# Differential attention on one core: context scores in the transpose and output banks

## The chip, the cores and the metric

One core of a Trainium2 chip runs the kernel. The metric is the device time of one execution in microseconds (us): the median of three runs of the kernel before is 1611.29 us (1610.94 to 1612.96).

## The reference

Two layers of a backbone with three token mixers in parallel. Each layer has 128 context tokens and 512 latent tokens, 640 columns in all. The mixer that the change touches is differential attention: 4 heads, each with two score maps of 64 channels,

```python
p = softmax(q1 k1 / 8) - lam * softmax(q2 k2 / 8)      # per head
o = p v
```

Context tokens read the 128 context keys only. Latent tokens read 512 latent and 256 cached keys, 768 in all. The output of a head then goes through an RMS norm per token. Beside it run a state-space mixer and a neighbourhood attention of 8 heads. All inputs are normalised and projected from one matrix, and the three results are merged by gates and projected again.

## The kernel before

Everything lies feature by token: 128 features on the partitions, 640 tokens along the free axis. Each float32 operand of a projection is split into a high and a low part and takes three matmuls (`feat`, line 163, matmul at line 175; a full projection of 128 features is 48 matmuls of 320 columns).

A layer runs the state-space mixer, then differential attention (`diff_attn`, line 496, once for each of 4 heads), then neighbourhood attention (`na_vkq`, `na_ctx`, `na_head`, 4 pairs of heads), then the last merges and the output projection. `build` (lines 1202 to 1233) puts projections that depend on none of these between the heads: keys and queries of the next head (`diff_kq`), a gate (`gate_in`), merge logits (`logits`, counts in `LA`, `LN`, `LC`), merges. Below they are called fill.

The order in which each engine gets its instructions is fixed at build time by a planner, which takes each engine's instructions by their place in the program as soon as they are ready in its own timeline. Tiles of one tag share that tag's buffers; a new tile waits until the one before it in the buffer is released.

PSUM has 8 banks. Three rotate for projections (tag `mm`, line 161). One bank, tag `t`, takes transposes; one, tag `o`, takes outputs (both from the pool `pp`). The last three are one tile, tag `s` (`bank3`, line 520), for the scores of a query tile: two maps of 768 columns.

A head goes like this. Context: scores of both maps into `s` (line 526); `soft` takes the maximum of both maps in one reduction (line 510), the exponentials (line 513, into the tiles `e0` and `e1`, one buffer each), and the difference of the maps (line 517); a transpose into `t` (line 529), its copy `px` (line 531), the output matmul into `o` (line 533), its copy into `of` (line 534). Then `after_ctx` runs `diff_out` of the previous head, which uses `o` twice (line 602). Then four latent query tiles: scores into `s` (lines 547 and 551), `soft`, two rounds of three transposes through `t` (line 558, copied at 560 and 561), and for each two query tiles 18 output matmuls into `o` (line 566), copied at line 568.

Between head h and head h+1 the program has `diff_norm` of head h (line 1212, body from line 571). It squares the head's output (line 576), sums the squares into `o` (line 201), makes the factor through VectorE and GpSimd, transposes it into the same `o` tile (line 591) and reads that at line 593, which is the tile's last reader. So in program order `o` goes: outputs of head h, `diff_norm` of head h, context output of head h+1, `diff_out` of head h.

Of the kernel before, what the change touches and what calls it, by code (L numbers as in the profile page):

```python
# [9 lines left out]
F32 = mybir.dt.float32  # L10
F32R = mybir.dt.float32r
AF = mybir.ActivationFunctionType
ALU = mybir.AluOpType
AX = mybir.AxisListType
# [110 lines left out]
class Net:  # L125
# [370 lines left out]
    def diff_attn(self, l, h, v, kq, nlam, p, cp, ps, pp, after_ctx):  # L496

        nc = self.nc
        half = (slice(0, 64), slice(64, 128))
        j = h % 2  # L500
        vh, vl, vx = v
        ks, qh, ql, kx, qx = kq
        of = cp.tile([128, NT], F32, tag="of", name="of", bufs=4)
        zz = cp.tile([128, 5, 2], F32, tag="zz", name="zz", bufs=2)

        def soft(s, n, t):

            st = p.tile([128, 4], F32, tag="st", name="st", bufs=3)
            e = [p.tile([128, 768], F32, tag=f"e{m}", name="e", bufs=1)[:, 0:n] for m in range(2)]
            nc.vector.tensor_reduce(out=st[:, 0:2], in_=s, axis=AX.X, op=ALU.max)  # L510
            nc.vector.tensor_scalar(out=st[:, 0:2], in0=st[:, 0:2], scalar1=-0.125, scalar2=None, op0=ALU.mult)  # L511
            for m in range(2):
                nc.scalar.activation(e[m], s[:, m], AF.Exp, bias=st[:, m:m + 1], scale=0.125, accum_out=zz[:, t, m:m + 1])  # L513
            nc.vector.reciprocal(st[:, 2:3], zz[:, t, 1:2])
            nc.vector.tensor_scalar(out=st[:, 3:4], in0=st[:, 2:3], scalar1=zz[:, t, 0:1], scalar2=nlam, op0=ALU.mult,
                                    op1=ALU.mult)
            nc.vector.scalar_tensor_tensor(out=e[0], in0=e[1], scalar=st[:, 3:4], in1=e[0], op0=ALU.mult, op1=ALU.add)
            return e[0]

        def bank3():  # L520
            return ps.tile([128, 1536], F32, tag="s", name="s")


        s = bank3().rearrange("p (b n) -> p b n", b=3)[:, 0:2, 0:128]
        for m in range(2):
            nc.tensor.matmul(s[:, m, :], lhsT=qx[half[m], :], rhs=kx[half[m], :], start=True, stop=True)
        e = soft(s, 128, 0)
        pt = pp.tile([128, 4, 128], F32, tag="t", name="t")
        nc.tensor.transpose(pt[:, 0, :], e, self.ident)
        px = p.tile([128, 128], F32, tag="px", name="px")  # L530
        nc.scalar.activation(px, pt[:, 0, :], AF.Copy)
        ov = pp.tile([128, 512], F32, tag="o", name="o")
        nc.tensor.matmul(ov[:, 0:128], lhsT=vx[:, j * 128:(j + 1) * 128], rhs=px, start=True, stop=True)
        nc.scalar.activation(of[:, 0:128], ov[:, 0:128], AF.Copy)
        after_ctx()

        for qp in range(2):
            ph = p.tile([128, 6, 256], F32R, tag="ph", name="ph")
            pl = p.tile([128, 6, 256], F32R, tag="pl", name="pl")
            for qi in range(2):  # L540
                qt = 2 * qp + qi
                s = bank3()
                qs = slice(qt * 128, (qt + 1) * 128)
                for m in range(2):
                    c0 = (512, 0)[m]
                    for i, q in enumerate((qh[m], ql[m])):
                        nc.tensor.matmul(s[:, m * 768 + c0:m * 768 + c0 + 256], lhsT=q[:, qs], rhs=ks[m][:, c0:c0 + 256],  # L547
                                         start=(i == 0), stop=(i == 1))
                    c0 = (0, 256)[m]
                    for i, q in enumerate((qh[m], ql[m])):  # L550
                        nc.tensor.matmul(s[:, m * 768 + c0:m * 768 + c0 + 512], lhsT=q[:, qs], rhs=ks[m][:, c0:c0 + 512],  # L551
                                         start=(i == 0), stop=(i == 1))
                e = soft(s.rearrange("p (m n) -> p m n", m=2), 768, 1 + qt)
                for b in range(2):
                    pt = pp.tile([128, 4, 128], F32, tag="t", name="t")
                    for i in range(3):
                        kt = 3 * b + i
                        nc.tensor.transpose(pt[:, i, :], e[:, kt * 128:(kt + 1) * 128], self.ident)  # L558
                    dst = (slice(None), slice(3 * b, 3 * b + 3), slice(qi * 128, qi * 128 + 128))
                    nc.scalar.activation(ph[dst], pt[:, 0:3, :], AF.Copy)  # L560
                    nc.vector.tensor_tensor(out=pl[dst], in0=pt[:, 0:3, :], in1=ph[dst], op=ALU.subtract)  # L561
            ov = pp.tile([128, 512], F32, tag="o", name="o")
            for kt in range(6):
                sv = slice(j * 128, (j + 1) * 128)
                for n, (x, q) in enumerate(((vh, ph), (vh, pl), (vl, ph))):
                    nc.tensor.matmul(ov[:, 0:256], lhsT=x[:, kt, sv], rhs=q[:, kt, :], start=(kt == 0 and n == 0),  # L566
                                     stop=(kt == 5 and n == 2))
            nc.scalar.activation(of[:, 128 + qp * 256:384 + qp * 256], ov[:, 0:256], AF.Copy)
        return of, zz
# [719 lines left out]
```

## Time and profile before

| what | value |
|---|---|
| median of 3 runs | 1611.29 us |
| the profiled execution's own time | 1611.84 us |
| its span | 1610.1 us |
| TensorE matmul busy | 1583.1 us, 98% |
| VectorE busy | 1064.1 us, 66% |
| ScalarE busy | 774.1 us, 48% |
| differential attention, layer 0 | about 252 to 484 us of the span |
| neighbourhood attention, layer 0 | about 487 to 731 us of the span |

Times in rows are microseconds from the span's start. PE is TensorE's matmul, ACT ScalarE, DVE VectorE, POOL GpSimd. A matmul's busy time includes the pipeline, so neighbouring matmuls overlap; the distance between their starts is what a matmul costs in a stream.

### The profile page before, as it was taken

What the parts mean: (1) busy time and instruction counts of PE and PEld (TensorE: products, weight loads), DVE (VectorE), ACT (ScalarE), POOL (GpSimd) and SP (SyncE); (2) the same over time, 40 slices, a digit from 0 to 9 for tenths busy, and PEclk for the clock granted to TensorE, in tenths of its full rate; (3) what the DMA queues carried; (4) which work ended last, traced back from release to release, by engine and by line L of the source; (5) the groups of instructions that cost most, each with busy time, mean ns of one, the idle gap of its engine ahead of it and who ended that gap; (6) DMA issues with size and microseconds to landing.
All of it is one profiled execution on the core that took longest, in us unless ns stands there. A gap on an engine that the chain in (4) does not pass through costs nothing.

```text
span 1610.1 us, 29172 instructions
## 1 busy us (share of the span) xinstructions
PE 1583.1 (98%) x11371; PEld 1508.3 (94%) x11371; DVE 1064.1 (66%) x2299; ACT 774.1 (48%) x1790; POOL 155.8 (10%) x182
## 2 busy tenths in 40 slices
PE   8999999999999999999999999999999999999998
PEld 5999899999999999999989989999999999999998
DVE  5865688667556566756677667676575575577565
ACT  4535654344445555443455466334444555454342
POOL 2003421011000000000000252101010000000000
PEclk9999999999999999999999999999999999999999
DMA  9663225321225343436543222452122543344543
GB/s 340 210 244 112 89 93 160 125 75 56 85 88 162 127 127 110 151 115 245 185 164 133 85 75 82 139 174 74 60 89 78 161 127 89 112 133 155 207 168 131
DMA packets 81673, 214.63 MB, mean 133 GB/s; under 512 B 9728, under 2 KB 25664, under 8 KB 80512
## 3 DMA queue, kind: packets, MB, share of 16 engines
q1 hardware_dynamic: 80624, 211.46, 40.1%
q8 instruction: 90, 1.47, 0.4%
q0 software_dynamic: 480, 0.88, 0.2%
q10 hardware_dynamic: 432, 0.43, 0.1%
q14 instruction: 47, 0.39, 0.1%
HBM read 170.27 MB, written 34.08 MB: 127 GB/s over the span
## 4 chain that ended last, share of the span: by engine, by line
PE 89%; DVE 4%; DMA 3%; ACT 1%; issue 1%; POOL 1%; SPq 0%; DVEq 0%; ACTq 0%; POOLq 0%
PE mm L175 61%; PE mm L187 7%; PE s L1001 2%; PE o L1025 2%; PE o L566 2%; PE t L1017 2%; PE ex L175 2%; PE s L551 1%; PE g L813 1%; PE t L558 1%; DMA aw<-in_w_ada 1%; PE y L826 1%; PE y L268 1%; PE s L547 1%; DMA qd<-qr 1%
## 5 line engine op out<-in xcount | busy, mean ns | idle before, releaser
L175 PE MATMUL mm<-hl,hi 128*128 128x320 f32 x1856 | 577.8, 311 | 0.8 <-DVE hl L383 0.8
L175 PE MATMUL mm<-hh,hi 128*128 128x320 f32 x1856 | 574.5, 310 | 3.3 <-ACT hh L382 2.8
L175 PE MATMUL mm<-hh,lo 128*128 128x320 f32 x1856 | 573.5, 309 | 0.2 <-DVE lo L151 0.2
L175 PEld LDWEIGHTS mm<-hh,hi 128*128 128x128 f32 x1856 | 348.4, 188 | 11.6 <-ACT hh L382 4.1
L175 PEld LDWEIGHTS mm<-hh,lo 128*128 128x128 f32 x1856 | 348.9, 188 | 7.3 <-issue 4.7
L175 PEld LDWEIGHTS mm<-hl,hi 128*128 128x128 f32 x1856 | 348.5, 188 | 6.3 <-issue 2.6
L151 DVE TENSOR_TENSOR lo<-raw,hi 128x1024 fp32r<-128x1024 f32 (+2 forms) x194 | 235.6, 1215 | 93.7 <-ACT hi L150 90.7
L150 ACT ACTIVATE hi<-raw 128x1024 fp32r<-128x1024 f32 (+2 forms) x194 | 200.1, 1032 | 177.5 <-PE mm L175 116.5
L175 PE MATMUL mm<-yh,hi 128*128 128x320 f32 x320 | 98.8, 311 | 1.1 <-DVE th L1080 0.7
L175 PE MATMUL mm<-yl,hi 128*128 128x320 f32 x320 | 99.0, 310 | 0.0
L175 PE MATMUL mm<-yh,lo 128*128 128x320 f32 x320 | 99.0, 310 | 0.0
L187 PE MATMUL mm<-hi,hh 128*128 128x264 f32 (+1 forms) x320 | 90.5, 284 | 1.8 <-DVE vl L423 1.7
L187 PE MATMUL mm<-lo,hh 128*128 128x264 f32 (+1 forms) x320 | 91.0, 285 | 0.0
L187 PE MATMUL mm<-hi,hl 128*128 128x264 f32 (+1 forms) x320 | 90.6, 284 | 0.0
L560 ACT ACTIVATE ph<-t 128x384 fp32r<-128x384 f32 x64 | 31.4, 490 | 113.9 <-PE t L558 113.9
L175 PE MATMUL mm<-mgh,hi 128*128 128x320 f32 x256 | 78.7, 311 | 1.7 <-ACT hi L150 1.7
L175 PE MATMUL mm<-mgl,hi 128*128 128x320 f32 x256 | 79.9, 312 | 0.0
L175 PE MATMUL mm<-mgh,lo 128*128 128x320 f32 x256 | 78.7, 309 | 1.0 <-DVE lo L151 1.0
L510 DVE TENSOR_REDUCE st<-s 128x2 f32<-128x1536 f32 (+1 forms) x40 | 59.5, 1487 | 25.6 <-PE s L551 24.0
L1018 ACT ACTIVATE ph<-t 128x512 fp32r<-128x512 f32 x64 | 38.3, 598 | 68.4 <-PE t L1017 68.0
L513 ACT ACTIVATE e<-s,st 128x768 f32<-128x768 f32 (+1 forms) x80 | 62.8, 795 | 15.1 <-DVE st L511 15.1
L561 DVE TENSOR_TENSOR pl<-t,ph 128x384 fp32r<-128x384 f32 x64 | 35.5, 554 | 49.9 <-ACT ph L560 49.4
(351 smaller groups left out, 3052.8 us busy)
## 6 DMA issues: line engine op xcount, KB each, us to landing
raw<-in_w_feat SPq DMA_DIRECT2D x110, 512.0 KB, 3.6
aw<-in_w_ada SPq DMA_DIRECT2D x8, 2048.0 KB, 8.2
raw<-in_w_out SPq DMA_DIRECT2D x32, 512.0 KB, 3.6
thd<-th SPq DMA_DIRECT2D x48, 320.0 KB, 2.2
th<-thd SPq DMA_DIRECT2D x48, 320.0 KB, 3.7
raw<-in_w_br SPq DMA_DIRECT2D x24, 512.0 KB, 3.5
accd<-th SPq DMA_DIRECT2D x32, 320.0 KB, 2.8
ac<-accd SPq DMA_DIRECT2D x32, 320.0 KB, 4.3
```

The costliest lines, as they stand in the source:

```text
L150: nc.scalar.activation(hi, raw, AF.Copy)
L151: nc.vector.tensor_tensor(out=lo, in0=raw, in1=hi, op=ALU.subtract)
L175: nc.tensor.matmul(ps, lhsT=s, rhs=r, start=(k == 0 and n == 0), stop=(k == K - 1 and n == 2))
L187: nc.tensor.matmul(ps, lhsT=s, rhs=r, start=(k == 0 and q == 0), stop=(k == 7 and q == 2))
L510: nc.vector.tensor_reduce(out=st[:, 0:2], in_=s, axis=AX.X, op=ALU.max)
L513: nc.scalar.activation(e[m], s[:, m], AF.Exp, bias=st[:, m:m + 1], scale=0.125, accum_out=zz[:, t, m:m + 1])
L561: nc.vector.tensor_tensor(out=pl[dst], in0=pt[:, 0:3, :], in1=ph[dst], op=ALU.subtract)
L566: nc.tensor.matmul(ov[:, 0:256], lhsT=x[:, kt, sv], rhs=q[:, kt, :], start=(kt == 0 and n == 0), stop=(kt == 5 and n == 2))
L1001: nc.tensor.matmul(s[:, c0:c0 + n], lhsT=q[:, i * 128:(i + 1) * 128], rhs=ks[j][:, k0:k0 + n], start=(x == 0), stop=(x == 1))
L1017: nc.tensor.transpose(pt[:, t, :], e[:, t * 128:(t + 1) * 128], self.ident)
L1018: nc.scalar.activation(ph[:, i], pt, AF.Copy)
L1025: nc.tensor.matmul(out, lhsT=lw, rhs=sel(q), start=(first and x == 0), stop=(last and x == 1))
```

## The change

The context scores of a head no longer use the three-bank tile `s`. Map 0 goes into a tile of tag `t`, map 1 into a tile of tag `o`. `soft` takes a list of two tiles in this case, and reduces each with an instruction of its own. Latent scores stay in `s`.

```diff
-            nc.vector.tensor_reduce(out=st[:, 0:2], in_=s, axis=AX.X, op=ALU.max)
+            if isinstance(s, list):
+                for m in range(2):
+                    nc.vector.tensor_reduce(out=st[:, m:m + 1], in_=s[m], axis=AX.X, op=ALU.max)
+            else:
+                nc.vector.tensor_reduce(out=st[:, 0:2], in_=s, axis=AX.X, op=ALU.max)
+                s = [s[:, m] for m in range(2)]
             nc.vector.tensor_scalar(out=st[:, 0:2], in0=st[:, 0:2], scalar1=-0.125, scalar2=None, op0=ALU.mult)
             for m in range(2):
-                nc.scalar.activation(e[m], s[:, m], AF.Exp, bias=st[:, m:m + 1], scale=0.125, accum_out=zz[:, t, m:m + 1])
+                nc.scalar.activation(e[m], s[m], AF.Exp, bias=st[:, m:m + 1], scale=0.125, accum_out=zz[:, t, m:m + 1])
...
-        s = bank3().rearrange("p (b n) -> p b n", b=3)[:, 0:2, 0:128]
+        s = [pp.tile([128, 512], F32, tag=t, name=t)[:, 0:128] for t in ("t", "o")]
         for m in range(2):
-            nc.tensor.matmul(s[:, m, :], lhsT=qx[half[m], :], rhs=kx[half[m], :], start=True, stop=True)
+            nc.tensor.matmul(s[m], lhsT=qx[half[m], :], rhs=kx[half[m], :], start=True, stop=True)
```

## Rows read from the trace of the kernel before

**Rows 1.** The page, part 1, TensorE: busy us, share of span, instructions.
```profile
PE 1583.1 (98%) x11371; PEld 1508.3 (94%) x11371; DVE 1064.1 (66%) x2299; ACT 774.1 (48%) x1790; POOL 155.8 (10%) x182
```

**Rows 2.** Windows of both layers' differential attention: window, length, busy us by engine.
```profile
250.00:460.00 210.00, 207.30 (x1452) 199.44 (x1451) 143.04 (x280) 95.62 (x199) 20.42 (x18) 1.00 0.33 100
...
1025.00:1260.00 235.00, 230.48 (x1601) 220.96 (x1600) 152.47 (x289) 101.48 (x212) 26.32 (x20) 1.00 0.31 97
```

**Rows 3.** Timeline, layer 0, head 0 to 1: start us, us, engine, line, operation.
```profile
325.79 0.39 ACT L568 ACTIVATE of<-o 128x256 f32<-128x256 f32 x1 [0.86 <-PE o L566]
326.07 0.27 ACT L531 ACTIVATE px<-t 128x128 f32<-128x128 f32 x1
326.23 0.74 ACT L576 ACTIVATE sq<-of 128x640 f32<-128x640 f32 x1
...
329.42 0.90 ACT L513 ACTIVATE e<-s,st 128x768 f32<-128x768 f32 x1 [2.45 <-DVE st L511]
...
331.83 1.02 DVE L517 SCALAR_TENSOR_TENSOR e<-e,st 128x768 f32<-128x768 f32 x1
...
335.50 0.49 PE L558 MATMUL t<-masks,e 128*128 128x128 f32 x3
...
337.23 0.55 DVE L561 TENSOR_TENSOR pl<-t,ph 128x384 fp32r<-128x384 f32 x1
...
339.73 0.49 PE L558 MATMUL t<-masks,e 128*128 128x128 f32 x3
...
339.93 0.81 DVE L593 TENSOR_TENSOR rows<-o,five 10x640 fp32r<-10x640 f32 x1 [0.96 <-PE o L591]
...
340.65 0.90 ACT L513 ACTIVATE e<-s,st 128x768 f32<-128x768 f32 x1
...
343.45 0.38 PE L533 MATMUL o<-px,vx 128*128 128x128 f32 x2
```

**Rows 4.** Timeline, layer 1, head 2 to 3, the last such place.
```profile
1220.15 0.38 ACT L568 ACTIVATE of<-o 128x256 f32<-128x256 f32 x1 [1.23 <-PE o L566]
...
1221.76 0.91 ACT L513 ACTIVATE e<-s,st 128x768 f32<-128x768 f32 x1 [0.43 <-DVE st L511]
...
1230.22 0.80 DVE L593 TENSOR_TENSOR rows<-o,five 10x640 fp32r<-10x640 f32 x1
...
1231.07 0.49 PE L533 MATMUL o<-px,vx 128*128 128x128 f32 x2 [0.17 <-DVE rows L593]
```

**Rows 5.** Timeline of TensorE, layer 1, context of head 2.
```profile
1154.90 0.49 PE L526 MATMUL s<-kx,qx 64*128 64x128 f32 x4
...
1158.53 0.27 PE L529 MATMUL t<-masks,e 128*128 128x128 f32 x1
```

**Rows 6.** One line's instructions: ns min/median/max, first and last start. Lines 510, 975.
```profile
L510 DVE TENSOR_REDUCE st<-s x40: 411/1751/1759, 253.3 to 1249.2; 128x2 f32<-128x1536 f32 x32, 128x2 f32<-128x256 f32 x8
...
L975 DVE TENSOR_REDUCE st<-s x16: 280/286/292, 487.9 to 1447.1; 128x1 f32<-128x128 f32 x16
```

**Rows 7.** Timeline of ScalarE, end of differential attention, layer 0.
```profile
464.03 0.43 ACT L1061 ACTIVATE th<-mm 128x320 f32<-128x320 f32 x1
466.49 0.28 ACT L892 ACTIVATE early<-mm 128x128 f32<-128x128 f32 x1 [2.03 <-PE mm L175]
...
484.46 0.39 ACT L568 ACTIVATE of<-o 128x256 f32<-128x256 f32 x1 [1.45 <-PE o L566]
```

**Rows 8.** Timeline of TensorE and VectorE, end of neighbourhood attention, layer 0.
```profile
719.02 0.60 PE L1017 MATMUL t<-masks,e 128*128 128x128 f32 x4
...
720.28 0.69 DVE L1019 TENSOR_TENSOR pl<-t,ph 128x512 fp32r<-128x512 f32 x1 [0.56 <-ACT ph L1018]
...
723.80 0.60 PE L1017 MATMUL t<-masks,e 128*128 128x128 f32 x4
...
725.13 0.30 PE L175 MATMUL mm<-yh,hi 128*128 128x320 f32 x1
...
727.77 0.39 PE L1025 MATMUL o<-ph,vs 128*128 128x512 f32 x1
```

**Rows 9.** One head's window by tile, `s`, `t`, `o` in turn; columns PE, PEld, DVE, ACT.
```profile
312.00:370.00 58.00, 7.08 (x36) 5.08 (x36) 7.42 (x5) 8.29 (x20) 1.00 0.27 81
312.00:370.00 58.00, 4.80 (x28) 3.37 (x28) 4.63 (x9) 4.70 (x10) 1.00 0.27 81
312.00:370.00 58.00, 7.83 (x51) 6.67 (x51) 2.04 (x4) 1.05 (x3) 1.00 0.27 81
```

**Rows 10.** Windows where the output projection starts: busy by engine, PEclk, DMA share.
```profile
764.00:768.00 4.00, 2.79 (x16) 2.00 (x14) 2.88 (x7) 2.98 (x5) 0.00 (x0) 1.00 0.29 96
768.00:780.00 12.00, 11.85 (x71) 11.85 (x72) 7.06 (x13) 4.12 (x6) 0.00 (x0) 0.86 0.58 182
```

## The prediction, as put on record before the result

> **What bounds the kernel now.** I read the page's table of engines first: TensorE is busy 98% of the span, the next engine 66% [rows 1]. So the time changes only if TensorE stands idle longer or shorter. The windows by stage come next: in the two stretches of differential attention TensorE idles 210.00 − 207.30 = 2.7 us and 235.00 − 230.48 = 4.5 us [rows 2]. That is 7.2 us for all that a shorter chain of heads could give back there.
>
> TensorE is full because fill stands between the steps of a serial chain: scores, softmax, transposes, outputs, tile after tile and head after head, then the same for neighbourhood attention. Differential attention's own matmuls are 7.08 + 4.80 + 7.83 = 19.7 us of a head's 58 us, about a third (a little less, since fill overlaps them) [rows 9]; the rest is fill. The reader must therefore look at two things: how long the chain is, and whether there is fill for its whole length.
>
> **What the change takes away.** Context scores no longer hold `s`, so the first latent scores of a head can be made, and their maxima taken, while the context softmax runs. What that can give is bounded by the 7.2 us of idle time and, below, by nothing; I put it at 0 alone, because today these scores wait little where TensorE has fill, and because of what comes next.
>
> **What it adds in instructions.** Eight context softmaxes (4 heads, 2 layers) reduce twice 286 ns instead of once 411 ns [rows 6]: 0.16 us each, 1.3 us of VectorE in all. VectorE is idle a third of the time; hidden, and at most 1.3 us if not. The score matmuls are the same.
>
> **What it adds in waits.** This is the large term. The score of map 1 now needs `o`. Between a head's last outputs and the next head's context the program gives `o` to `diff_norm`. That buffers of a tag go round in program order is to be read from the trace: at the first change of heads `o` is copied out from 325.79 to 326.18, the context's `px` is there at 326.34, and the squares that `diff_norm` sums are there only at 326.97; yet the context output (line 533) runs at 343.45, after the norm's last reader (339.93 + 0.81 = 340.74) [rows 3]. At the last change TensorE even stands still before line 533 until line 593 is done [rows 4]. Of six such changes (heads 0 to 1, 1 to 2, 2 to 3, two layers) these are the first and the last. Today this costs nothing: the context output is not in the chain, and the head's latent tiles go on. After the change the *scores* of the context wait there, and behind them the context softmax; and since `e0` and `e1` have one buffer each, the first latent exponential waits behind the context's transpose. Behind line 526 on TensorE's queue stand the fill and the first latent scores; the planner can put them ahead of it, so that the wait is the chain's and not the queue's. Who waits is ScalarE, with the exponentials, and through them every later tile of the head. No DMA is added or moved.
>
> The price of one change of heads, from the end of the output copy to the first latent exponential:
> - Today: 329.42 − 326.18 = 3.2 us at the first [rows 3], 1221.76 − 1220.53 = 1.2 us at the last [rows 4].
> - Afterwards: `o` is held for 340.74 − 326.18 = 14.6 us [rows 3] down to 1231.02 − 1220.53 = 10.5 us [rows 4]. Then the context: from its scores to the end of its transpose 1158.80 − 1154.90 = 3.9 us, where nothing was in the way [rows 5], with 0.2 us for the second reduction. Then 0.4 us until the exponential, as from the transposes' end at 340.22 to 340.65 [rows 3]; its maxima are ready.
> - So longer by at least 10.5 + 3.9 + 0.2 + 0.4 − 3.2 = 11.8 us and at most 14.6 + 4.5 − 1.2 = 17.9 us. I take the middle, 15 us: with the softmax out of the way VectorE serves the norm sooner, but the norm's five small steps and its two trips over TensorE remain.
>
> Three changes of heads in a layer: the chain is 45 us longer (35 to 54). The first head of a layer has no norm before it and costs nothing.
>
> **What covers it.** TensorE goes on with fill that the program has later. But the fill of differential attention ends with the last logit at 464.03; at 466.49 TensorE is already in the projections of neighbourhood attention, while the last head's output is copied at 484.46 [rows 7]. And what is taken from there is missing at the end of neighbourhood attention, where there is none over: the logits run out at 725.13, when the first merge operand appears, 2.6 us before the chain's last outputs at 727.77 [rows 8]. So in each layer some 45 us of fill are lacking in all, at the end of differential or of neighbourhood attention.
>
> **What the lack costs.** Not 45 us, because the chain is quicker where no fill stands in it. One tile takes 340.65 − 329.42 = 11.2 us from exponential to exponential. Of these, the first transposes start 2.65 us after their input (332.85 to 335.50) and the second 1.95 us after theirs (337.78 to 339.73) [rows 3]: by itself the tile would take 6.6 us, 0.6 of it. In neighbourhood attention transposes are 4.8 us apart and the second stand ready from 720.97, 2.8 us early [rows 8], so by that step 0.4; I use 0.6 for both. If 45 us of fill are two thirds of a stretch, the stretch is 67 us long as it is spaced now; by itself 0.6 x 67 = 40 us; TensorE's own work in it is 22 us; idle 18 us. The chain enters each of the two stretches some 2.5 us ahead of TensorE (the delays above), which takes off 5 us: 13 us in a layer, 26 us in all.
>
> Ends: 35 us lacking at 0.5 gives 26 − 17 − 5 = 4 us in a layer, 8 in all; 54 us at 0.8 gives 65 − 27 − 5 = 33 us, 66 in all. Added to the profiled execution's 1611.84 us the forecast is 1638; its time is 0.55 us above the median of the runs, so I put 1637 us, with its own range 1619 to 1660.
>
> **A rule on the clock.** At the start of the output projection TensorE is busy 2.79 of 4 us, and in the next 12 us its granted clock averages 0.86, so part of them was at the lower level, 1.2 GHz, against 2.4 GHz before [rows 10]. The Trainium skill, TensorE: Matmul & The Clock Gate, section Part 1: The HAM clock gate, says that the slower clock is what an engine gets that has lately had little to do. By that rule, with which these rows agree, stretches without fill run at half clock; it is the second rival below.
>
> **Rivals.**
> 1. *The delays swallow it.* The chain's lead of 2 to 3 us at every TensorE step [rows 3, 8] might absorb the lack all along, since order and not latency rules a full engine. For it: TensorE waits hardly at all today. Against: at the last change of heads it did wait for the norm [rows 4], so there the lead was used up. Time 1608 to 1614.5.
> 2. *Half clock.* TensorE's 22 us of own work in the stretches become 44 us, more than the 40 us of the chain: 22 us lost in a layer, with no lead to take off, 44 in all: 1655 us. If nothing at all were hidden, 2 x 54 = 108 us: 1719. For it: the rows just named. Against: idle and busy alternate in such a stretch, and a slower TensorE fills itself.
> 3. *Faster: the freed `s` decides.* If the planner gives `o` to the context's scores before the norm, they run at once and latent scores stand ready behind them; the chain gets shorter and TensorE's idle 7.2 us [rows 2] shrink: 1604 to 1608 us. It decides as soon as `o` does not go round in program order. Against: the two changes of heads shown.
> 4. *Nothing happens*: the norm gets so quick without the softmax beside it that `o` is free when the context comes. It would have to fall from 10.5 us to about 2; one GpSimd step and two trips over TensorE lie in it. I count this with the first.
>
> **How the numbers follow.** Forecast (a longer chain, partly uncovered) 0.54; rival 2 0.13; rivals 1 and 4 0.18; rival 3 0.15. What a measurement here can tell from no change is 0.2%, 3.2 us. Slower: 0.54 + 0.13 = 0.67; same 0.18; faster 0.15. The range for 8 in 10 goes from 1607, which leaves out about half of rival 3, to 1668, which leaves out the upper half of rival 2 and the tail of the forecast.
>
> **What would show it.** In the changed kernel: line 526 comes after line 593 at the six changes of heads, and the first latent exponential some 16 us after the copy of the outputs, not 1 to 3; line 547 of a head's first tile comes before or beside line 526; the last logits are done before the last transposes of neighbourhood attention, with bare gaps between transposes there; TensorE's busy time about the same and its idle time 20 to 30 us longer, in the last third of differential attention and at the end of neighbourhood attention. The prediction is wrong if line 526 comes before line 593, or if it comes after and TensorE's idle time does not grow.

## The result, and the profile after

The changed kernel takes 1673.95 us (median of 4 runs, 1671.71 to 1676.5) against 1611.12 us of the kernel before beside it: a ratio of 1.0385, with an interval of 1.0372 to 1.0399. It is 62.8 us slower. The direction and the wait for the bank `o` were forecast, the size was not: 1637 us was predicted, 1668 us was the upper end.

Lines behind the change are numbered 5 higher than before (526 is now 531, 568 is 573, 593 is 598, 513 is 518); the second reduction is line 512, the latent one 514.

Part 1 of the page, which answers to [rows 1]: busy us, share of the span, instructions.

```profile
PE 1613.6 (96%) x11371; PEld 1530.1 (91%) x11371; DVE 1069.5 (64%) x2307; ACT 774.7 (46%) x1790; POOL 158.5 (9%) x182
```

The span is 1673.5 us, 63.4 longer. The same 11371 matmuls are busy 30.5 us longer, and TensorE stands still 59.9 instead of 27.0 us, 32.9 more. So the loss has two halves, and the reader must look for both.

The first change of heads in layer 0, from the timeline of the changed kernel; it answers to [rows 3].

```profile
323.95 0.49 PE L531 MATMUL t<-kx,qx 64*128 64x128 f32 x2
...
324.06 0.38 ACT L573 ACTIVATE of<-o 128x256 f32<-128x256 f32 x1 [2.23 <-PE o L571]
...
324.48 0.74 ACT L581 ACTIVATE sq<-of 128x640 f32<-128x640 f32 x1
...
324.69 1.75 DVE L514 TENSOR_REDUCE st<-s 128x2 f32<-128x1536 f32 x1
...
328.41 1.17 PE L201 MATMUL o<-masks,sq 128*128 128x1 f32 x10
...
336.75 0.81 DVE L598 TENSOR_TENSOR rows<-o,five 10x640 fp32r<-10x640 f32 x1
...
338.02 0.48 PE L531 MATMUL o<-kx,qx 64*128 64x128 f32 x2
...
339.49 0.36 ACT L518 ACTIVATE e<-o,st 128x128 f32<-128x128 f32 x1
...
342.19 0.27 PE L534 MATMUL t<-masks,e 128*128 128x128 f32 x1
...
343.52 0.27 ACT L536 ACTIVATE px<-t 128x128 f32<-128x128 f32 x1
...
343.68 0.91 ACT L518 ACTIVATE e<-s,st 128x768 f32<-128x768 f32 x1
```

The predicted order stands there step by step. The maxima of the first latent tile are taken at 324.69 (line 514), and its exponential waits until 343.68: behind the norm's last reader (336.75), the score of map 1 (338.02), the context softmax and its transpose (342.19). From the end of the output copy (324.44) that is 19.2 us; before it was 3.2. It is so at all six changes: map 1 goes into `o` 10 to 17 us after map 0 into `t`, and each time after the norm's last reader. The line's instructions, two for each change; first and last start:

```profile
L531 PE MATMUL t<-kx,qx x12: 272/322/374, 324.0 to 1272.5; 64*128 64x128 f32 x12
...
L531 PE MATMUL o<-kx,qx x12: 272/322/373, 338.0 to 1284.4; 64*128 64x128 f32 x12
```

From the end of the copy to the first latent exponential the six changes take 19.2, 22.7, 14.0, 20.3, 22.0 and 18.0 us; before they took 3.2, 1.2, 2.4, 3.1, 3.8 and 1.2. That is 16.9 us more on average. I call this the wait at a change of heads; the experiments are compared by the sum of the six, which rises from 14.9 to 116.3 us.

Now where TensorE loses. Windows of layer 0 from the first head's context on, cut at the start of head 1's context, at the first neighbourhood score and at the last outputs; columns as in [rows 2]. First the kernel before:

```profile
252.00:312.00 60.00, 59.73 (x411) 58.21 (x410) 44.40 (x85) 25.07 (x50) 3.24 (x4) 1.00 0.50 155
312.00:487.40 175.40, 172.97 (x1223) 166.24 (x1222) 108.63 (x206) 81.38 (x174) 17.18 (x14) 1.00 0.27 84
487.40:731.00 243.60, 243.60 (x1728) 238.11 (x1728) 153.40 (x386) 123.58 (x317) 2.73 (x2) 1.00 0.41 129
```

Then the kernel after, cut at the same events:

```profile
252.00:324.00 72.00, 72.00 (x499) 70.46 (x498) 53.22 (x103) 29.57 (x57) 7.00 (x7) 1.00 0.47 147
324.00:514.50 190.50, 175.94 (x1163) 165.60 (x1162) 101.27 (x188) 75.97 (x163) 15.97 (x12) 0.96 0.22 67
514.50:761.50 247.00, 242.85 (x1702) 236.61 (x1702) 154.78 (x389) 124.94 (x321) 2.71 (x2) 0.99 0.41 131
```

The layer is 509.5 − 479.0 = 30.5 us longer for the same work, 3364 against 3362 matmuls. TensorE's idle time rises from 0.27 + 2.43 + 0 to 0 + 14.56 + 4.15, by 16.0 us. The other 14.5 us are busy time: a matmul in 324.0 to 514.5 takes 175.94 / 1163 = 0.1513 us instead of 0.1414. Of this the slower clock, shown next, can be at most 10.2 us: 20.5 us of the layer were at the lower level, none before. No run splits the rest. Only 26 of 1728 matmuls moved from neighbourhood attention to differential attention.

Part of why the same matmuls are slower shows at the end of head 1, in TensorE's timeline of the changed kernel:

```profile
371.75 0.49 PE L563 MATMUL t<-masks,e 128*128 128x128 f32 x3
373.75 0.55 PE L563 MATMUL t<-masks,e 128*128 128x128 f32 x3 [1.51 <-DVE pl L566]
376.64 0.39 PE L552 MATMUL s<-ks,qh 128*128 128x256 f32 x1 [2.34 <-ACT e L518]
...
382.00 0.41 PE L571 MATMUL o<-ph,vl 128*128 128x256 f32 x1
...
387.34 1.69 PE L201 MATMUL o<-masks,sq 128*128 128x1 f32 x10 [2.05 <-ACT sq L581]
...
389.24 0.41 PE L187 MATMUL mm<-lo,hh 128*128 128x256 f32 x1
...
395.21 0.31 PE L175 MATMUL mm<-hh,lo 128*128 128x320 f32 x1
```

and in windows of the stretch with the first two gaps, of the stretches behind them and behind the third, and of one behind a single gap of 1.90 us at 448.39; the third column from the end is the granted clock:

```profile
371.75:376.64 4.89, 1.04 (x8) 0.56 (x6) 2.79 (x6) 2.75 (x6) 0.00 (x0) 1.00 0.00 0
376.60:385.00 8.40, 7.76 (x33) 6.50 (x34) 2.57 (x5) 1.19 (x3) 0.00 (x0) 0.59 0.00 0
...
387.34:396.00 8.66, 8.66 (x46) 8.61 (x46) 4.51 (x14) 2.39 (x3) 1.17 (x1) 0.61 0.09 20
...
450.29:458.50 8.21, 8.05 (x51) 7.42 (x52) 3.13 (x5) 2.15 (x4) 0.00 (x0) 1.00 0.31 106
```

Between and behind the transposes of a tile TensorE has nothing (1.51 and 2.34 us), and after the outputs it waits for the squares (2.05 us). Behind these gaps it works at 1.2 GHz most of the time: an output matmul takes 0.21 us from start to start and not 0.12, and so does each matmul of the value projection until 394. Not every gap has this behind it: the clock stayed at 2.4 GHz behind the single gap of 1.90 us, and in the kernel before behind one of 1.72 us at 375.26. What stands before the fall at 377.8 is 4.89 us in which TensorE was busy for 1.04. Over the execution 63.3 us are at the lower level, against 10.6 before; at half speed that is at most 26.4 of the 30.5 us of longer busy time. The Trainium skill, TensorE: Matmul & The Clock Gate, section Part 1: The HAM clock gate, has the slower clock follow on little activity; the first two windows agree.

What TensorE waits for, in the changed kernel: us in total, times, longest.

```profile
PE s L552 <- ACT e L518: 10.3, 6, 2.3
PE mm L175 <- ACT th L1066: 5.2, 8, 1.3
PE o L201 <- ACT sq L581: 4.1, 3, 2.0
...
PE t L563 <- DVE pl L566: 3.2, 3, 1.5
```

The first, third and fourth are short waits of the chain's own steps, next to which no fill was ready; the first was 1.7 us in all before. The second is of projections that wait until ScalarE has read an earlier result out of a bank. The wait of map 1 itself is hardly among them (1.0 us), since the fill goes on there.

### The profile page after: what moved, and what is told of

Same layout as the page of the kernel before. It is cut to its first block, busy times and chain, and to the rows that moved or that the text cites. A ratio compares the mean times of both kernels' runs of the same rounds, so it can differ in the third digit from the quotient of the medians.

```text
span 1673.5 us, 29181 instructions
## 1 busy us (share of the span) xinstructions
PE 1613.6 (96%) x11371; PEld 1530.1 (91%) x11371; DVE 1069.5 (64%) x2307; ACT 774.7 (46%) x1790; POOL 158.5 (9%) x182
## 4 chain that ended last, share of the span: by engine, by line
PE 90%; DVE 3%; ACT 3%; DMA 3%; issue 1%; POOL 0%; SPq 0%; DVEq 0%; ACTq 0%; POOLq 0%
PE mm L175 61%; PE mm L187 7%; PE o L571 2%; PE s L1006 2%; PE o L1030 2%; PE t L1022 2%; PE s L556 2%; PE ex L175 2%; PE t L563 1%; DMA aw<-in_w_ada 1%; PE g L818 1%; PE y L831 1%; PE s L552 1%; PE y L268 1%; ACT e L518 1%
## 5 line engine op out<-in xcount | busy, mean ns | idle before, releaser
L565 ACT ACTIVATE ph<-t 128x384 fp32r<-128x384 f32 x64 | 31.3, 490 | 122.3 <-PE t L563 122.3
L566 DVE TENSOR_TENSOR pl<-t,ph 128x384 fp32r<-128x384 f32 x64 | 35.4, 553 | 59.8 <-ACT ph L565 59.3
L514 DVE TENSOR_REDUCE st<-s 128x2 f32<-128x1536 f32 x32 | 56.1, 1753 | 27.3 <-PE s L556 27.1
L187 PEld LDWEIGHTS mm<-hi,hh 128*128 128x128 f32 x320 | 62.4, 195 | 2.3 <-ACT th L1066 1.5
```

What stands on the lines that cost most here:

```text
L187: nc.tensor.matmul(ps, lhsT=s, rhs=r, start=(k == 0 and q == 0), stop=(k == 7 and q == 2))
```

## The experiments

Eleven kernels were run, each beside runs of the kernel before, against whose median its time is taken here. Beside it stands the sum of the six waits at a change of heads, in one profiled execution of each. It goes with the large losses at about one rate; the small ones it does not order. Two profiles of the changed kernel differ by 3 us in it:

| kernel | sum of six waits, us | more than before | time over the kernel before, us | per us of wait |
|---|---|---|---|---|
| before | 14.9 | | | |
| norm late, old banks | 16.5 | 1.6 | 6.8 | 4 |
| two reductions, old banks | 21.1 | 6.2 | 5.0 | 0.8 |
| projection banks | 28.8 | 13.9 | 17.3 | 1.2 |
| values unblocked, old banks | 34.1 | 19.2 | 15.2 | 0.8 |
| `t` and `s` | 52.9 | 38.0 | 21.2 | 0.56 |
| norm behind the context | 59.8 | 44.9 | 29.2 | 0.65 |
| values unblocked | 111.4 | 96.5 | 60.8 | 0.63 |
| the change, again | 113.3 | 98.4 | 60.9 | 0.62 |
| busy in the gaps | 115.1 | 100.2 | 64.2 | 0.64 |
| the change | 116.3 | 101.4 | 62.8 | 0.62 |
| logits earlier | 122.3 | 107.4 | 73.1 | 0.68 |
| `s` and `o` | 150.5 | 135.6 | 70.2 | 0.52 |

**Norm behind the context.** The changed kernel with the norm of heads 0 to 2 put behind the next head's context, so that map 1 finds `o` free.

```diff
-                                d = self.diff_norm(att, cp, pp)
+                                d = self.diff_norm(att, cp, pp) if h == 3 else None
...
-                                pend.append(lambda ...: self.diff_out(l, h, att, d, g, sg, pp))
+                                pend.append(lambda ...: self.diff_out(l, h, att, self.diff_norm(att, cp, pp) if d is None else d, g, sg, pp))
```

> The changed kernel, with the norm of heads 0 to 2 placed behind the next head's context (just ahead of its output step) and not ahead of it; banks as changed. Theory A, the context scores wait for the output bank behind the norm: line 531 comes right after the head's last outputs, the first latent exponential 5 to 8 us after the output copy instead of 19 to 24, and the time falls from 1674 to 1600 to 1615 us. Rival B, the transpose bank held by a context map, or two reductions, or the freed three-bank tile itself cost the time: 1650 us or more.

1643.32 us, a ratio of 1.0183 (1.0165 to 1.0201). Between the two expectations: with the norm out of the way about half of the loss goes, not all. A wait of 8 to 12 us stays at each change of heads.

**One bank each.** Which of the two banks costs?

```diff
-        s = [pp.tile([128, 512], F32, tag=t, name=t)[:, 0:128] for t in ("t", "o")]
+        s = [pp.tile([128, 512], F32, tag="t", name="t")[:, 0:128], bank3()[:, 512:640]]
```

> The changed kernel, with context map 0 in the transpose bank and map 1 in the three-bank score tile; nothing waits for the output bank. Theory A: 1606 to 1617 us, as before the change. Rival B, the transpose bank is what costs: 1650 us or more.

```diff
+        s = [bank3()[:, 0:128], pp.tile([128, 512], F32, tag="o", name="o")[:, 0:128]]
```

> The changed kernel, with context map 0 in the three-bank score tile and map 1 in the output bank. Theory A: the whole loss stays, or more, since the score tile is now held while the norm runs: 1665 to 1695 us. Rival B, the transpose bank: 1606 to 1617 us.

With `t` and `s` 1635.36 us, 1.0137 (1.0121 to 1.0153); with `s` and `o` 1684.36 us, 1.0434 (1.0403 to 1.0466). The second met its first theory, the first missed both: with no wait for `o` a loss of 21 us remains. Its timeline at the first change of heads:

```profile
326.55 0.48 PE L531 MATMUL t<-kx,qx 64*128 64x128 f32 x2
...
326.66 0.38 ACT L573 ACTIVATE of<-o 128x256 f32<-128x256 f32 x1 [0.72 <-PE o L571]
...
328.57 0.37 ACT L518 ACTIVATE e<-t,st 128x128 f32<-128x128 f32 x1 [0.76 <-DVE st L516]
...
337.43 0.90 ACT L518 ACTIVATE e<-s,st 128x768 f32<-128x768 f32 x1 [0.38 <-DVE st L516]
```

Map 0 needs `t` back from the previous head's last transposes (read until 323.35), so the context starts where the head before ends. In the kernel before it had been done beside that head's last tile:

```profile
312.11 0.49 PE L526 MATMUL s<-kx,qx 64*128 64x128 f32 x4
```

This wait the prediction did not see. And with map 1 in `s` the latent scores are late again, which is what the change had meant to avoid, so the 21 us are not the price of `t` alone. The timeline of `s` and `o`:

```profile
325.36 0.39 ACT L573 ACTIVATE of<-o 128x256 f32<-128x256 f32 x1 [0.72 <-PE o L571]
...
337.75 0.81 DVE L598 TENSOR_TENSOR rows<-o,five 10x640 fp32r<-10x640 f32 x1 [0.37 <-PE o L596]
...
340.72 0.48 PE L531 MATMUL o<-kx,qx 64*128 64x128 f32 x2
...
349.62 0.90 ACT L518 ACTIVATE e<-s,st 128x768 f32<-128x768 f32 x1 [0.17 <-DVE st L516]
```

Here `s` is held until map 1 has come, the latent scores follow that, and the wait is 23.9 us. That is 7 to 9 us more time than the full change takes, in which `s` is free but map 0 waits for `t`; the two are not parted here.

**Logits earlier.** If fill lacks at the changes of heads, more of it there should help.

```diff
-LA = ((), (1, 2), (3,), (4, 5, 6))
+LA = ((), (1, 2, 3, 4), (), (5, 6))
```

> The changed kernel, with logits 3 and 4 of the first merge placed at head 1, ahead of the second value projection, instead of at heads 2 and 3. In the changed kernel TensorE has no fill from 371.9 to 388.9 us: value columns fill the three projection banks and wait for the value tile that head 1 still reads. Theory C, fill is there but blocked at that place: two more logits (14 us of matmuls) ahead of the block shorten the time by 8 to 25 us, to 1649 to 1666. Rival D, fill is lacking in total and it only moves: 1670 to 1680 us.

1687.3 us, 1.0451 (1.0424 to 1.0479), 10 us more over the kernel before than the change, and outside both expectations. The lack moved: the half clock of 378 to 395 is gone but for 3.4 us, and 10.2 us of it stand behind 513.9. In all TensorE is idle for 66.0 us and at half clock for 76.1. Only the place of fill was changed, not its amount. Why the time grew by 10 us is not shown.

**Projection banks.** Scores in two of the three rotating banks, so that neither `t` nor `o` is needed.

```diff
+        s = [self.bank()[:, 0:128] for _ in range(2)]
```

> The changed kernel, with both context maps in projection banks (each map in one of the three that rotate); the context waits neither for the transpose bank nor for the output bank, and the three-bank tile is free for latent scores. If the two waits are the whole loss, which is theory A with the transpose bank added (6 us of chain per change of heads by the run with the transpose bank and the score tile): 1604 to 1618 us. If the projection banks, which go round in program order, block fill for as long as a context map sits in them: 1625 us or more.

1630.78 us, 1.0102 (1.0087 to 1.0117). Four of the six waits fall to 0, but at the change from head 1 to 2 the context gets its banks only behind the value projections, and the wait is 14.3 us in both layers:

```profile
378.35 0.38 ACT L573 ACTIVATE of<-o 128x256 f32<-128x256 f32 x1
...
383.33 0.49 PE L531 MATMUL mm<-kx,qx 64*128 64x128 f32 x4
...
393.02 0.90 ACT L518 ACTIVATE e<-s,st 128x768 f32<-128x768 f32 x1
```

The time is in the range of the second expectation. The six waits, only 13.9 us longer than before, do not account for all of the 17 us. Of the four other placements it is the cheapest, and it still loses: in each one a bank has a user whom the context then waits for.

**Norm late, old banks.** The kernel before with the edit of the first experiment, to see what that edit costs by itself.

> The kernel before, with nothing changed but the norm of heads 0 to 2 placed behind the next head's context. Theory A: the output bank is not in the chain of the kernel before, so 1606 to 1617 us. If the place of the norm by itself costs (the second half of the loss in the run where it was moved in the changed kernel): 1625 us or more.

1620.32 us, 1.0038 (1.0023 to 1.0053): 6 to 7 us, between the expectations. If that price is the same in the changed kernel, some 7 of the 29 us that stayed in the first experiment belong to the late norm; no run shows the sum.

**Values unblocked.** In the changed kernel the second value projection sits finished in its three banks until head 1's outputs are done, and TensorE has no projection to run from 371.9 to 388.9. Here those banks are emptied at once; what is left out is the second pair's values, since heads 2 and 3 read the first pair's.

```diff
-                                    v = self.diff_v(l, 1, vp)
+                                    v = self.diff_v_free(l, 1, vp, v)
```

> The changed kernel, with the second value projection computed and copied out to scratch, and heads 2 and 3 reading the first pair's values: its columns no longer wait in the projection banks for head 1 to end (TensorE had no fill from 371.9 to 388.9 us there). Theory C, the missing fill is blocked at that place: 1640 to 1662 us, and no stretch of half clock about 378 to 395 us. Theory D, what counts is that the chain is longer than its fill: 1666 to 1680 us, with the idle time elsewhere.

The same edit in the kernel before:

> The kernel before with the same edit of the second value projection (heads 2 and 3 read the first pair's values), as a control: 1604 to 1613 us by either theory, since TensorE stood still there only about 2 us a layer.

The changed kernel: 1674.27 us, 1.0379 (1.0362 to 1.0395), no better. The kernel before: 1628.64 us, 1.0093 (1.0077 to 1.011), 15 us worse, which neither theory had: with the new order of fill two of its waits are 9.8 us long. In the changed kernel the granted clock is better (44.3 us at half clock), yet what was gained in busy time came back as idle time:

```profile
PE 1606.3 (96%) x11371; PEld 1522.4 (91%) x11371; DVE 1065.4 (64%) x2305; ACT 773.2 (46%) x1788; POOL 158.9 (10%) x182
```

Its span is 1671.4 us: busy 7.3 us less than in the change, idle 5.2 us more. So the second theory's range is met. But the same edit costs 15 us in the kernel before, so it may have given back as much as it cost: between the two edited kernels lie 45.6 us, not 61 to 63. That the blocked values have no part in the loss is not shown.

**Two reductions.** The changed kernel with its scores back in two banks of `s`: of the change only the second reduction is left.

```diff
+        s3 = bank3()
+        s = [s3[:, 0:128], s3[:, 512:640]]
```

> The changed kernel, but with its context scores in two banks of s, as in the kernel before; what is left of the change is the second reduction, 8 times 0.16 us. By my prediction's first term it is hidden: 1609 to 1614 us. By the rival that VectorE's part of a context stands on the chain it is at most 1.3 us times the spacing of fill, 1612 to 1616. Over 1620 would mean that something else than the banks costs.

1617.49 us, 1.003 (1.0018 to 1.0043), 5 us and not 1.3: just above both ranges. The waits of layer 0 are unchanged; in layer 1 the one at the change from head 1 to 2 grows from 3.8 to 8.4 us, and the next from 1.2 to 2.7. The timeline of this kernel there:

```profile
1158.22 0.49 DVE L512 TENSOR_REDUCE st<-s 128x1 f32<-128x128 f32 x2 [0.42 <-PE s L532]
...
1158.95 0.37 ACT L518 ACTIVATE e<-s,st 128x128 f32<-128x128 f32 x1 [1.74 <-DVE st L516]
...
1160.15 0.38 ACT L574 ACTIVATE of<-o 128x256 f32<-128x256 f32 x1
...
1160.94 0.39 ACT L518 ACTIVATE e<-s,st 128x128 f32<-128x128 f32 x1
```

The same pair of exponentials in the kernel before:

```profile
1156.17 0.37 ACT L513 ACTIVATE e<-s,st 128x128 f32<-128x128 f32 x1 [1.73 <-DVE st L511]
...
1156.53 0.36 ACT L513 ACTIVATE e<-s,st 128x128 f32<-128x128 f32 x1
```

The pair of reductions takes 0.49 us; the single one takes 0.42 at this place. But the second map's exponential now stands behind five other instructions in ScalarE's order, 1.99 us after the first; before, it followed after 0.36. So the longer wait comes with another order of the planner's, not with the 0.07 us of the instruction.

**Busy in the gaps.** The changed kernel with 92 useless matmuls in the gaps of head 1, to bring the clock back.

```diff
+                    for _ in range({(1, 2, 0): 12, (1, 2, 1): 18, (1, 3, 0): 4}.get((h, qt, b), 0)):
+                        nc.tensor.transpose(pt[:, 3, :], e[:, 0:128], self.ident)
...
+            for _ in range(12 if h == 1 and qp == 1 else 0):
+                nc.tensor.matmul(ov[:, 256:512], lhsT=vh[:, 5, sv], rhs=ph[:, 5, :], start=True, stop=True)
```

> The changed kernel with useless matmuls where TensorE stands still late in head 1 of both layers: 12, 18 and 4 beside the transposes of its third and fourth tile, in unused columns of t, and 12 after its last outputs, in unused columns of o: 92 in all, at 0.117 us each 10.8 us of work, some 10 us of it in stretches where TensorE was idle. In the changed kernel about 6.8 us at half clock follow these gaps in layer 0 (from 377.8 and again from 388.0) each time, 4 and 7 us in layer 1. Theory A, that half of the loss is TensorE at half clock: with the gaps filled those 25 us run at the full clock, the outputs and projections in them take 12 us less, and the time falls by 5 to 12 us: 1661 to 1668 us, with at most 45 us at half clock in the trace. Theory B, that the chain alone sets the time and the clock only fills what is idle anyway: 1671 to 1680 us, although the clock is back.

> The changed kernel as it is, beside the two others so that differences of a few us can be told: 1670 to 1677 us by either theory.

1676.7 us, 1.0393 (1.0378 to 1.0407), beside 1673.39 us, 1.0379 (1.0361 to 1.0396), for the change run again: no gain. At half clock there are 52.8 us, more than the 45 that the first theory asked for. The windows that answer to the two stretches:

```profile
381.20:389.60 8.40, 7.49 (x50) 6.24 (x50) 2.56 (x5) 1.18 (x3) 0.00 (x0) 1.00 0.00 0
...
391.80:400.60 8.80, 8.79 (x57) 8.73 (x58) 5.83 (x15) 2.39 (x3) 1.17 (x1) 0.81 0.17 51
```

The first stretch is back at 2.4 GHz, with 16 useless matmuls more in the same 8.4 us, and the second partly. But the copies of the transposes now come after the useless matmuls in their tile, and the tile before takes 12.0 us instead of 9.0. What the clock gave back, the longer chain may have taken. The time fits the second theory, but it is no clean test: the clock and the chain were changed together.

## Why the prediction was wrong

**Right.** Map 1 waits for the norm at all six changes; the chain is longer by 16.9 us on average (11.6 to 21.5), forecast 15 (11.8 to 17.9). The latent scores and maxima are there early. TensorE's idle time grows by 32.9 us, forecast 26 (8 to 66); that the size is near is in part luck: half of it was forecast for the end of neighbourhood attention, where there is none, and it was worked out with a quickening of the tiles that did not come.

**The step that failed is "What the lack costs".** It made 45 us of longer chain in a layer into 13 us of time, 0.29. Measured are 101.4 / 2 = 50.7 us and 62.8 / 2 = 31.4 us, 0.62, and about the same rate, 0.52 to 0.68, holds in all eight kernels whose chain was lengthened by 38 us or more; five of these are the changed kernel with its banks and norm as they are, so they are not eight separate proofs. Two things are wrong in it.

First, it counts idle time alone. The prediction's start says that the time changes only if TensorE stands idle longer or shorter; it takes a slower TensorE as a rival that excludes the forecast, and its own list says "TensorE's busy time about the same". Measured are 30.5 us more busy time for the same matmuls beside 32.9 us more idle time. The longer busy time belongs into the sum: 14.5 us in layer 0, at most 10.2 of them by the clock. That "a slower TensorE fills itself" is what the stretch from 389 to 394 contradicts, where projections simply take nearly twice as long. With this busy time beside the forecast's idle time, 26 + 2 x 14.5 = 55 us, the sum would have come to 1666 us. Whether the lower clock costs time by itself stays open: in two kernels with less of it (44.3 and 52.8 us) the time did not fall, but both had other changes.

Second, it lets the chain run at 0.6 of its spacing in two stretches of 67 us. The tiles did not quicken like that: in layer 0 they regain 7.5 us of 49.2 (the last tile's exponentials start at 509.8 against 468.1, 41.7 later). Another 14.6 us come back at neighbourhood attention's first score: its query projection, copied 14.4 us after those exponentials before (482.51), is copied 9.6 us ahead of them now (500.21). So 27.1 us are left at that score (514.5 against 487.4), and 30.5 at its end.

The range is too narrow by the prediction's own sum as well. Its ends are 8 and 66 us, which give 1619 and 1677 us; it writes 1660 for the second. The measured time lies inside those ends, but by a busy time that they do not hold.

**"What covers it" was wrong about where the lack would be.** It had TensorE take fill from later, so that it is missing at the end of neighbourhood attention. Only 26 matmuls, 3.7 us, were taken from there, and its last 17.5 us are full:

```profile
521.00:528.00 7.00, 5.21 (x27) 4.98 (x25) 4.89 (x13) 6.21 (x19) 0.00 (x0) 0.76 0.87 264
...
545.00:553.00 8.00, 5.74 (x32) 4.89 (x32) 7.18 (x23) 4.09 (x13) 1.54 (x1) 0.79 0.15 33
553.00:745.00 192.00, 192.00 (x1364) 187.95 (x1363) 121.90 (x305) 96.89 (x246) 0.00 (x0) 1.00 0.39 125
745.00:762.50 17.50, 17.50 (x124) 17.31 (x123) 6.96 (x14) 6.70 (x14) 0.00 (x0) 1.00 0.41 139
```

Neighbourhood attention loses its 4 us at its start: 1.8 us while a projection waits for ScalarE to copy values, and 2.3 us in the window at 545, where nothing stands beside the chain. The rest of the loss is in heads 1 to 3. The 88 more matmuls before head 1's context were not made sooner: up to 324.0 us both kernels have made the same number since 252, 497 and 499. The context had moved back by 12 us, and the fill that ran meanwhile was missing in heads 1 to 3.

**"What it adds in waits" missed the wait of map 0 for `t`.** In the kernel with `t` and `s`, where nothing waits for `o`, there are 38 us more of waits and 21 us more of time, part of it by `s`. In the full change it lies in front of the wait for `o`, so the size of the chain term came out right.

**"What it adds in instructions" priced the second reduction at nothing to 1.3 us.** It came with 5 us, and with a changed order on ScalarE.

**The rivals.** Half clock (1655, to 1719) was the nearest, and its rows, the clock of 0.86 behind a gap [rows 10], were the right ones. The delays did not swallow it, `o` goes round in program order, and the norm got quicker by 1.4 us only, at the first change of heads: from the squares to its last reader's end it takes 337.56 − 324.48 = 13.1 us, and 14.5 before [rows 3].

## What to carry to other kernels

Before a tile is moved to another buffer, write down who else rotates through that buffer, and add the longest holder's time to the chain of the one that moves: here each of four other placements of the context scores was dearer than the three banks they blocked. Where TensorE is full because fill stands beside a chain, price a longer chain as idle time plus longer busy time, not as one or the other: here it was 32.9 and 30.5 us. And in an order made by a planner an edit that was forecast at nothing or 1 us can bring 5 or 15 us with a changed order, so a small term needs its own run.

## What was not expected of the hardware

The granted clock fell (0.59 and 0.61 in stretches of 8.4 and 8.7 us) behind gaps of 1.5 to 2.4 us, although TensorE was busy 96% of the span; behind single gaps of 1.90 and 1.72 us it did not fall. So the length of one gap does not tell what follows it: before the first fall TensorE had been busy for 1.04 of 4.89 us. And two runs with less half clock were not faster: at 44.3 us instead of 63.3 the busy time was 7.3 us less and the idle time 5.2 us more.
